# Second unit's weight splits and mixed operands queued behind the first half's normalisation, and the forget gates' chain moved to a later down product, in a hybrid decoder trunk

## The chip, the core and the metric

One NeuronCore of a Trainium2 chip runs the whole program in one launch. The metric is the device time of one execution in microseconds (us). Engines: PE (TensorE, matmul), DVE (VectorE), ACT (ScalarE), POOL (GpSimd), and SP (SyncE), which here only issues DMAs.

## What is computed

Sixteen learned meta tokens and 512 input tokens, 528 in all, of width D = 1024 pass through two layers; each has three steps, and each step ends in a LayerNorm of (scaled residual + new part). All is float32.

```
for l in range(2):
    h = layer_norm(ALPHA*h + 0.5*swiglu(h, ffn1_wg[l], ffn1_wu[l], ffn1_wd[l]), ...)
    mix = short_conv(h, ...) if l == 0 else forgetting_attention(h, w_q, w_o, k, v, c)
    h = layer_norm(ALPHA*h + mix, ...)
    h = layer_norm(ALPHA*h + 0.5*swiglu(h, ffn2_wg[l], ffn2_wu[l], ffn2_wd[l]), ...)
    if l == 0: k, v, c = shared_kv(h, kv_w, f_bias)  # c = cumsum(log_sigmoid(h @ w_f + f_bias))
```

`swiglu(x) = (silu(x @ wg) * (x @ wu)) @ wd` has 2816 inner columns. `short_conv` multiplies one projection of x by a 3-tap convolution of the product of two others. The attention has 8 heads of 128; its scores get c[query] - c[key] added before the softmax.

## The kernel before

**Layout.** The residual `y` stays in SBUF, transposed: features on the partitions (8 blocks of 128), tokens along the free axis. Tokens are worked on in two halves, h = 0 and 1, of 264 columns each (256 in layer 1, where the meta tokens are gone).

**Exact products.** A float32 product is made of three fast ones. Each operand is split in a high part (rounded, `wh`, `xh`) and the rest (`wl`, `xl`); `gemms` (L232) issues wl·xh, wh·xl and wh·xh for each block of 128 features and then calls `tick()`, which runs what `later(n, ...)` has put off by n such ticks. For weights ACT makes `wh` (a copy, L127) and DVE makes `wl` (a subtraction, L129) in `split_w`; for activations ACT and DVE do the same in `split_x` (L250). Weights are loaded by SP into three `raw` buffers of 1 MB and split into five pairs `wh`, `wl`; the first tiles of some stages have homes of their own (`xtile`) so that they can be made early.

**FFN stages.** A `Quads` holds a pair of 256-column blocks of wg and wu, cut into quarters a11 to a22. A `Unit` (L507) computes the pair for both halves at once with seven products p1 to p7 in place of eight (a Strassen form), from sums of weight quarters (`Quads.sums`, L186: s, s2, s3 on DVE; s4 at L205) and mixed operands t1 to t4 of the activations (`Mixed.sums`, L308, on DVE and ACT). These need both halves of the tokens. So the first unit after a norm can be `Direct` (L571): eight plain products, half 0 first, then half 1, with two activations each out of PSUM (`sg`, L648). `run_units` (L592) runs the Direct unit's two halves, then p1, p2, p5 and so on of the second unit. Direct first units stand at the start, in the second FFN of both layers, and in the keys and values; the first FFN of layer 1 follows the keys without a norm between. `finish` ends a unit, `down` (L477) multiplies by wd and adds to `y`.

**Norm.** `Norm.pre` takes the first feature block as a shift (`first`, a matmul, `shift` six ticks later); `add` adds each down product to `y` (L495, DVE), squares it (L400, ACT; three buffers `sq`) and accumulates sums and squares on POOL (L404, L406). `post(h)` runs for each half a few ticks after its last block: two matmuls (L414) sum over the partitions into `pd` and `pv`, then `finish`, under a priority higher than what is traced around it, runs a chain on DVE: variance (L425), an inverse root by iterations (`rsqrt`, L345 to L353), then for each pair of blocks a multiply and an add (L433, L434, DVE), gain and bias (L437, ACT) and the split (`self.to.made`, L251 and L252). The last `xl` goes into the list `newest`.

**What sets the order.** TensorE's instructions run as they are traced (`manual_schedule`). The order of DVE, ACT, POOL and SP is made at build time by the Tile scheduler: of the instructions whose inputs are there, the one traced first, with the norm's chain ahead. `behind()` (L111) holds an instruction until the newest `xl` traced so far has been issued; every `wl` and every weight sum is made under it:

```
def behind():
    return tc.issue_after(newest[-1].ins) if newest else nullcontext()
```

Within `down` of a stage with a norm, `ahead()` (at n == 2*LEAD) splits the next stage's first weights before the norm begins: a11, a21, a12, a22 of the Direct unit, blocks 0 of w_in[1] and w_in[2] for the convolution, q_w(0) and q_w(1) for the queries. In `post`, once half 1's finish is traced, `self.to.sums()` follows: for a `Mixed` the second unit's a11, a12 and s1 and all of t1 to t4; for a `Plain` (the inputs of the convolution and the queries) nothing.

**Stages in order.** Start (transposes of x, first FFN of layer 0), convolution (`conv_u`, `conv_b`, written out for the first two blocks as (u,0,0), (u,1,0), (b,0,0), (u,0,1), (b,0,1), (u,1,1), (b,1,0), (b,1,1), where a u is 48 matmuls and a b is 24), its down product, second FFN, keys and values (`kv_direct`, L833, then units), in whose second unit `gates` (L844) runs the whole chain of the forget gates (8 x 528 elements on DVE, L874 to L888, then the store of `c_dram` on POOL's queue), first FFN of layer 1, queries (`project`: heads 0 to 2 and 3, 4 for half 0, then 0 to 2 for half 1) and attention, its down product, last FFN with the output norm. `turn_c` turns c into columns for the scores, 160 ticks after the keys.

## Time and profile before

| | |
|---|---|
| median of 3 runs | 1967.3 us (1965.5 to 1967.4) |
| the profiled execution: time / span | 1965.4 / 1963.6 us |
| TensorE busy | 1886.4 us, 96%, 14467 matmuls |
| VectorE / ScalarE / GpSimd busy | 1401.3 (71%) / 876.1 (45%) / 133.6 us (7%) |
| mean granted TensorE clock | 0.985 of full speed |
| chain that ended last, by engine | PE 86%, DVE 9%, ACT 2%, issue, DMA and POOL 1% each |
| HBM traffic | 96 GB/s over the span |

The span runs from the first to the last instruction of the profiled execution; the device time has about 2 us around it. A row of an engine "in order of time" gives the start, the duration, the line, the tiles (written <- read), their shapes and, in brackets, the engine's idle time before it and what ended that. In the tables of waits an idle time is put down to the event that came last.

### The profile page before, as it was taken

The numbers are of one execution on the slowest core, as the hardware profiler recorded it, in microseconds if no ns is written. First come the engines' busy times: TensorE is split into PE (matmuls) and PEld (weight loads), VectorE is DVE, ScalarE is ACT, GpSimd is POOL, SyncE is SP. The second block draws the span as 40 slices with busy tenths as digits, with TensorE's granted clock in tenths as the row PEclk, the third lists the DMA queues.
The fourth block names the chain that finished last, engine by engine and source line by source line (L and its number), as shares of the span: only waits on it lengthen the run. The fifth ranks groups of instructions, "written<-read, shape, count | busy, mean of one in ns | idle before, by whom it ended". The sixth has DMA issues, their size and how long they took to land.

```text
span 1963.6 us, 34602 instructions
## 1 busy us (share of the span) xinstructions
PE 1886.4 (96%) x14467; PEld 1822.4 (93%) x14467; DVE 1401.3 (71%) x2077; ACT 876.1 (45%) x1459; POOL 133.6 (7%) x198
## 2 busy tenths in 40 slices
PE   8999999979998999999899999999979989999997
PEld 7999999879998999999899998989968888989897
DVE  6686767754478776767899875858658787858685
ACT  5353535433245353535454453535435544535360
POOL 0000000400031000000421000000300220000000
PEclk9999999989999999999999999999979999999999
DMA  4333323222230332323233323333413302333241
GB/s 143 119 99 96 108 87 108 65 97 84 100 97 18 123 108 87 108 87 110 85 110 131 108 89 105 98 101 109 146 54 116 102 1 97 103 109 102 96 130 44
DMA packets 180682, 190.43 MB, mean 97 GB/s; under 512 B 5834, under 2 KB 174070, under 8 KB 180526
## 3 DMA queue, kind: packets, MB, share of 16 engines
q1 hardware_dynamic: 178510, 182.74, 29.1%
q0 software_dynamic: 2016, 5.49, 0.8%
q8 instruction: 113, 1.85, 0.4%
q14 instruction: 43, 0.35, 0.1%
HBM read 181.76 MB, written 6.44 MB: 96 GB/s over the span
## 4 chain that ended last, share of the span: by engine, by line
PE 86%; DVE 9%; ACT 2%; issue 1%; DMA 1%; POOL 1%; SPq 0%; DVEq 0%; ACTq 0%; POOLq 0%
PE pb L238 26%; PE pc L238 15%; PE pa L238 6%; PE pcv L238 2%; PE pcc L238 2%; PE pcb L238 2%; PE pq L238 2%; DVE wl L129 1%; DVE xl L252 1%; DVE y L433 1%; DVE y L434 1%; PE psc L953 1%; PE po L1011 1%; ACT y L437 1%; PE pt L708 0%
## 5 line engine op out<-in xcount | busy, mean ns | idle before, releaser
L129 DVE TENSOR_TENSOR wl<-raw,wh 128x1024 fp32r<-128x1024 f32 (+1 forms) x440 | 518.8, 1185 | 201.2 <-ACT wh L127 187.1
L127 ACT CAST wh<-raw 128x1024 fp32r<-128x1024 f32 (+1 forms) x440 | 439.2, 1003 | 480.9 <-PE pc L238 74.0
L238 PE MATMUL pb<-xh,wl 128*128 128x264 f32 (+1 forms) x1408 | 400.8, 285 | 11.0 <-ACT sg L648 11.0
L238 PE MATMUL pb<-xh,wh 128*128 128x264 f32 (+1 forms) x1408 | 400.2, 284 | 0.0
L238 PE MATMUL pb<-xl,wh 128*128 128x264 f32 (+1 forms) x1408 | 400.0, 284 | 0.0
L238 PE MATMUL pc<-xh,wl 128*128 128x264 f32 (+1 forms) x960 | 273.8, 285 | 7.4 <-DVE wl L129 6.4
L238 PEld LDWEIGHTS pb<-xh,wl 128*128 128x128 f32 x1408 | 266.9, 190 | 11.8 <-ACT sg L648 11.4
L238 PE MATMUL pc<-xl,wh 128*128 128x264 f32 (+1 forms) x960 | 272.9, 284 | 3.4 <-DVE xl L252 3.4
L238 PE MATMUL pc<-xh,wh 128*128 128x264 f32 (+1 forms) x960 | 272.4, 284 | 0.0
L238 PEld LDWEIGHTS pb<-xh,wh 128*128 128x128 f32 x1408 | 267.8, 190 | 0.0
L238 PEld LDWEIGHTS pb<-xl,wh 128*128 128x128 f32 x1408 | 266.9, 190 | 0.3
L238 PEld LDWEIGHTS pc<-xh,wl 128*128 128x128 f32 x960 | 181.4, 189 | 8.4 <-DVE wl L129 3.9
L238 PEld LDWEIGHTS pc<-xl,wh 128*128 128x128 f32 x960 | 181.5, 189 | 4.5 <-DVE xl L252 4.5
L238 PEld LDWEIGHTS pc<-xh,wh 128*128 128x128 f32 x960 | 181.8, 189 | 0.0
L238 PE MATMUL pa<-xh,wl 128*128 128x264 f32 (+1 forms) x352 | 99.7, 283 | 0.0
L238 PE MATMUL pa<-xh,wh 128*128 128x264 f32 (+1 forms) x352 | 99.6, 283 | 0.0
L238 PE MATMUL pa<-xl,wh 128*128 128x264 f32 (+1 forms) x352 | 99.5, 283 | 0.0
L127 ACT CAST wh<-s 128x1024 fp32r<-128x1024 f32 x44 | 46.1, 1047 | 48.4 <-DVE s L194 7.9
L238 PEld LDWEIGHTS pa<-xh,wh 128*128 128x128 f32 x352 | 66.3, 188 | 0.0
L238 PEld LDWEIGHTS pa<-xh,wl 128*128 128x128 f32 x352 | 66.2, 188 | 0.0
L238 PEld LDWEIGHTS pa<-xl,wh 128*128 128x128 f32 x352 | 66.2, 188 | 0.0
L437 ACT ACTIVATE y<-y,vecs 128x264 f32<-128x264 f32 (+1 forms) x80 | 43.9, 597 | 45.1 <-DVE y L434 45.1
(1919 smaller groups left out, 4558.5 us busy)
## 6 DMA issues: line engine op xcount, KB each, us to landing
raw<-in_ffn_wg_dram SPq DMA_DIRECT2D x88, 512.0 KB, 3.8
raw<-in_ffn_wu_dram SPq DMA_DIRECT2D x88, 512.0 KB, 4.8
raw<-in_ffn_wd_dram SPq DMA_DIRECT2D x48, 768.0 KB, 4.5
raw<-in_conv_w_in_dram SPq DMA_DIRECT2D x12, 1024.0 KB, 4.9
raw<-in_ffn_wd_dram SPq DMA_DIRECT2D x16, 512.0 KB, 3.6
raw<-in_kv_w_dram SPq DMA_DIRECT2D x16, 512.0 KB, 4.7
raw<-in_conv_w_out_dram SPq DMA_DIRECT2D x4, 1024.0 KB, 5.4
raw<-in_attn_w_q_dram SPq DMA_DIRECT2D x4, 1024.0 KB, 6.7
```

Source lines behind the costliest of these rows:

```text
L127: nc.scalar.copy(a, src)
L129: nc.vector.tensor_tensor(b, src, a.bitcast(F32), ALU.subtract)
L238: nc.tensor.matmul(ps, lhsT=a[:, k, :], rhs=b(k), start=start and k == ks[0] and j == 0, stop=stop and k == ks[-1] and j == 2, skip_group_ ...
L252: return nc.vector.tensor_tensor(dst_l, src32, dst_h.bitcast(F32), ALU.subtract)
L433: nc.vector.tensor_tensor(ym, ym, rb, ALU.mult)
L434: nc.vector.tensor_tensor(ym, ym, bb, ALU.add)
L437: nc.scalar.activation(yv[:, j, :], yv[:, j, :], AF.Identity, scale=vecs[:, c:c + 1], bias=vecs[:, 48 + c:49 + c])
L953: nc.tensor.matmul(ps, lhsT=q[:, M + t * P:M + (t + 1) * P], rhs=kt[:, a:b], start=True, stop=True)
L1011: nc.tensor.matmul(po[:, q0:S], lhsT=vt[:, j * P:(j + 1) * P], rhs=pT[j // 2][:, j % 2, q0:S], start=j == 0, stop=False)
```

## The change

1. `behind()` takes the instructions to wait for; `split_x` returns ACT's copy and DVE's subtraction.
2. `Norm.post` calls `self.to.early()` after half 0's finish in place of `self.to.sums()` after half 1's. For a `Mixed`, `early` makes the second unit's a11, a12 and the weight sums (with a11 split before the sums overwrite it); for the convolution it splits w_in[1](1), w_in[2](1) and w_in[0](0), for the queries heads 2, 3 and 4.
3. `Mixed.sums` (t1 to t4 and the split of s1) is called by `run_units` between the Direct unit's two halves, behind the last split pair of half 0's output (in the keys behind ACT's last copy); t3 is split at once, t4 is written in t2's place. `turn_x` no longer calls it at the start. For this, `ready` becomes a list of two `Quads`.
4. `shift` comes eight ticks after `first`, not six, and `sq` has four buffers, not three.
5. The gates' chain becomes `forget()`, 232 ticks after the gates' matmuls; it works in `c_keep` and copies the result there at the end. `turn_c` comes 320 ticks after the keys, not 160.

```diff
...
@@ -108,9 +108,14 @@
     newest = []
-    def behind():
-
-        return tc.issue_after(newest[-1].ins) if newest else nullcontext()
+    @contextmanager
+    def behind(*after):
+
+
+        with ExitStack() as stack:
+            for ins in after or newest[-1:]:
+                stack.enter_context(tc.issue_after(ins.ins))
+            yield
     def split_w(src, shape, home=None):
@@ -186,6 +191,7 @@
         def sums(self):
             if "s" in self.got:
                 return
+            self("a11")
             s = wp.tile([P, KD * P], F32, tag="ws", bufs=1, name="s")
             s = s.rearrange("p (j k n) -> p j k n", j=2, k=KH)
             self.got["s"] = s
@@ -248,16 +254,17 @@
             finish()
     def split_x(dst_h, dst_l, src32):
-        nc.scalar.copy(dst_h, src32)
-        return nc.vector.tensor_tensor(dst_l, src32, dst_h.bitcast(F32), ALU.subtract)
+        a = nc.scalar.copy(dst_h, src32)
+        return a, nc.vector.tensor_tensor(dst_l, src32, dst_h.bitcast(F32), ALU.subtract)
     class Plain:
-        def __init__(self, layer):
+        def __init__(self, layer, early):
             self.layer = layer
             self.q = {}
+            self.early = early
         def made(self, h, m):
@@ -270,9 +277,6 @@
             k = m % KH
             return split_x(a[:, k:k + 2, :w], b[:, k:k + 2, :w], yv[:, m:m + 2, :])
-        def sums(self):
-            pass
-
         def operands(self, h):
             w = SPAN[self.layer][h][1]
             return tuple(
...
@@ -305,15 +309,19 @@
             i, k = m // KH, m % KH
             return split_x(*self.tiles(f"b{i + 1}{h + 1}", k), self.part(i, h, k))
+        def early(self):
+
+
+            self.left("a11")
+            self.left("a12")
+            self.left.sums()
+
         def sums(self):
-
             b = self.part
             w = self.w
             new = lambda n: gtile(n, 2 * w).rearrange("p (k c) -> p k c", k=2)
             t = {}
-            self.left("a11")
-            self.left("a12")
             for k in range(0, KH, 2):
                 t1 = new("t1")
                 nc.vector.tensor_tensor(t1, b(0, 0, k), b(0, 1, k), ALU.subtract)
@@ -324,13 +332,11 @@
                 nc.vector.tensor_tensor(t3, b(1, 1, k), b(0, 1, k), ALU.subtract)
                 nc.vector.scalar_tensor_tensor(t2, b(0, 0, k), -1.0, t3, ALU.mult, ALU.subtract)
                 split_x(*self.tiles("t2", k), t2)
-                t[k] = t2, t3
+                split_x(*self.tiles("t3", k), t3)
+                t[k] = t2
             for k in range(0, KH, 2):
-                split_x(*self.tiles("t3", k), t[k][1])
-            for k in range(0, KH, 2):
-                t4, t2 = new("t4"), t[k][0]
-                nc.vector.scalar_tensor_tensor(t4, t2, -1.0, b(1, 0, k), ALU.mult, ALU.subtract)
-                split_x(*self.tiles("t4", k), t4)
+                nc.vector.scalar_tensor_tensor(t[k], t[k], -1.0, b(1, 0, k), ALU.mult, ALU.subtract)
+                split_x(*self.tiles("t4", k), t[k])
         def __getitem__(self, name):
             if name == "b12":
@@ -385,7 +391,7 @@
                 for m, gather in self.early.pop(h, ()):
                     self.add(h, m, gather)
-            later(6, shift)
+            later(8, shift)
         def add(self, h, m, gather):
@@ -396,7 +402,7 @@
             yv = cols(y, h, self.layer)
             if m == 1:
                 self.s1[h] = self.tmp(h, "s1")
-            sq = self.tmp(h, "sq", 3)
+            sq = self.tmp(h, "sq", 4)
             nc.scalar.activation(sq, yv[:, m, :], AF.Square)
             if m == KD - 1:
                 self.sq[h] = sq
@@ -414,8 +420,8 @@
                     nc.tensor.matmul(ps, lhsT=ones_all, rhs=t, start=n == 0, stop=n == 1)
             with tc.high_priority(offset=SOON):
                 self.finish(h, pd, pv)
-            if h == 1:
-                self.to.sums()
+            if h == 0:
+                self.to.early()
         def finish(self, h, pd, pv):
             yv = cols(y, h, self.layer)
@@ -438,7 +444,7 @@
                         yv[:, j, :], yv[:, j, :], AF.Identity,
                         scale=vecs[:, c:c + 1], bias=vecs[:, 48 + c:49 + c])
                 last = self.to.made(h, m)
-            newest.append(last)
+            newest.append(last[1])
     def lagged(n, head, layer, group=1, tail=0):
@@ -584,7 +590,8 @@
                         gemms([(ps[j, m], (wh[:, j], wl[:, j]), self.xs[f"b{n + 1}{h + 1}"])],
                               range(KH), start=n == 0, stop=n == 1, chained=True)
             for m in range(2):
-                finish(m, h, ps[0, m], ps[1, m])
+                last = finish(m, h, ps[0, m], ps[1, m])
+            return last
     def first_four(quads):
         return lambda: [quads(n) for n in ("a11", "a21", "a12", "a22")]
@@ -594,9 +601,12 @@
         if direct:
-            units[0].xs.left = units[1].quads
+            xs = units[0].xs
             for h in range(2):
-                units[0].half(h, direct)
+                last = units[0].half(h, direct)
+                if h == 0:
+                    with behind(*last):
+                        xs.sums()
             if after:
                 after(0)
         i0 = int(direct is not None)
...
@@ -647,14 +660,13 @@
                 sg = gtile("sg", w)
                 nc.scalar.activation(sg, pg, AF.Silu)
                 nc.vector.tensor_tensor(sg, sg, pu, ALU.mult)
-                split_h(m, h * w, sg)
+                return split_h(m, h * w, sg)
             units = []
             for i in range(fn // 2):
                 c0 = (f0 + 2 * i) * P
-                fresh = ready and not (c or i)
-                q = ready if fresh else Quads([a[:, c0:c0 + 256] for a in (wg, wu)])
-                if not fresh:
+                q = ready[i] if ready and c == 0 else pair_quads(wg, wu, c0)
+                if not ready or c or i:
                     units.append(Unit(q, xs, [lambda m: gtile("g"), lambda m: gtile("u")]))
                 else:
                     units.append(Direct(q, xs))
...
@@ -712,9 +725,6 @@
             nc.scalar.copy(y[:, m, c0:c0 + w], ps[:, :w])
             if m % 2:
                 xs0.made(h, m - 1)
-        if h == 1:
-            xs0.sums()
-
     def turn_vecs():
         ps = psum("pvec")
         nc.tensor.transpose(out=ps[:, :120], in_=vr, identity=ident[:120, :120])
@@ -726,11 +736,11 @@
     later(8 * KD, turn_vecs)
-    xc = Plain(0)
     w_in = [Weights(conv_w_in[0], 0, KD, j * D, KD) for j in range(3)]
     for j in (1, 2):
         w_in[j].home = {0: xtile}
-    ffn(0, ffn1_wg[0], ffn1_wu[0], ffn1_wd[0], 0, xs0, xc, ready=first,
+    xc = Plain(0, lambda: (w_in[1](1), w_in[2](1), w_in[0](0)))
+    ffn(0, ffn1_wg[0], ffn1_wu[0], ffn1_wd[0], 0, xs0, xc, ready=f1,
         ahead=lambda: (w_in[1](0), w_in[2](0)))
     zh, zl = {}, {}
@@ -790,15 +800,15 @@
         o, w = SPAN[0][h]
         return (lambda k: zh[k][:, o:o + w]), (lambda k: zl[k][:, o:o + w])
-    xs1 = Mixed(0)
-    f2 = Quads([a[0][:, :256] for a in (ffn2_wg, ffn2_wu)], xtile)
+    f2 = [pair_quads(ffn2_wg[0], ffn2_wu[0], c, None if c else xtile) for c in (0, 256)]
+    xs1 = Mixed(0, f2[1])
     down(0, Weights(conv_w_out[0], 0, KD, 0, KD), KD, z_operands, True,
-         Norm(0, 1, EPS, xs1), ALPHA, ahead=first_four(f2))
-
-    xs2 = Mixed(0)
+         Norm(0, 1, EPS, xs1), ALPHA, ahead=first_four(f2[0]))
+
     kv_quads = [
         Quads([kv_w[:, j * D + i * 256:j * D + (i + 1) * 256] for j in range(2)], None if i else xtile)
         for i in range(H // 2)]
+    xs2 = Mixed(0, kv_quads[1])
     ffn(0, ffn2_wg[0], ffn2_wu[0], ffn2_wd[0], 2, xs1, xs2, ready=f2, ahead=first_four(kv_quads[0]))
@@ -835,9 +845,10 @@
         for j, ps in enumerate(pss):
             if h == 0:
                 kv0[j, m] = htile("kvT", F32)
-            nc.scalar.copy(kv0[j, m][:, o:o + w], ps)
+            last = nc.scalar.copy(kv0[j, m][:, o:o + w], ps)
         if h == 1:
             kv_store(0, m, kv0[0, m], kv0[1, m])
+        return [last]
     c_keep = nrm.tile([H, T], F32, name="c_keep")
@@ -858,7 +869,7 @@
         nc.vector.tensor_tensor(fl[:, :, 0:H], fr, fh[:, :, 0:H].bitcast(F32), ALU.subtract)
         nc.vector.tensor_scalar(fn[:, :, 0:H], fh[:, :, 0:H].bitcast(F32), -1.0, None, ALU.mult)
         nc.vector.tensor_scalar(fm[:, :, 0:H], fl[:, :, 0:H].bitcast(F32), -1.0, None, ALU.mult)
-        z, e, q, q2, acc = (gtile(n)[:H] for n in ("z", "e", "q", "q2", "acc"))
+        z = c_keep
         low = lambda a, b: (a[:, :KH], b[:, :KH])
         high = lambda a, b: (a[:, KH:], b[:, KH:])
@@ -870,6 +881,11 @@
             for n, (wt, name) in enumerate(parts):
                 gemms([(ps, wt, xs2[name])], range(KH), start=n == 0, stop=n == len(parts) - 1)
             nc.vector.tensor_scalar(z[:, o:o + w], ps[:H, :], fbias, None, ALU.add)
+        later(29 * KD, forget)
+
+    def forget():
+        z = c_keep
+        e, q, q2, acc, c = (gtile(n)[:H] for n in ("e", "q", "q2", "acc", "c"))
         nc.scalar.activation(e, z, AF.Abs)
         nc.scalar.activation(e, e, AF.Exp, scale=-1.0)
@@ -884,7 +900,8 @@
         nc.vector.tensor_scalar(z, z, 0.0, None, ALU.min)
         nc.vector.scalar_tensor_tensor(z, acc, -2.0, z, ALU.mult, ALU.add)
         nc.vector.memset(e, 1.0)
-        nc.vector.tensor_tensor_scan(c_keep, e, z, 0.0, ALU.mult, ALU.add)
+        nc.vector.tensor_tensor_scan(c, e, z, 0.0, ALU.mult, ALU.add)
+        nc.vector.tensor_copy(z, c)
         nc.gpsimd.dma_start(c_dram, c_keep)
     kv_units = []
@@ -901,12 +918,12 @@
                 out=pt[:, :H], in_=c_keep[:, M + t * P:M + (t + 1) * P], identity=ident[:H, :H])
             nc.vector.tensor_copy(cqT[:, t, :], pt[:, :H])
-    later(20 * KD, turn_c)
-
-
-    xq = Plain(1)
+    later(40 * KD, turn_c)
+
+
     q_w = Weights(attn_w_q[0], 0, KD, 0, H)
     q_w.home = {m: xtile for m in range(2)}
+    xq = Plain(1, lambda: [q_w(m) for m in range(2, 5)])
     ffn(1, ffn1_wg[1], ffn1_wu[1], ffn1_wd[1], 3, xs2, xq, ahead=lambda: (q_w(0), q_w(1)))
     opened = {}
...
```

## Rows read from the trace of the kernel before

**Rows 1.** Busy time by stretch: start:end length, PE, PEld, DVE, ACT, POOL, clock, DMA, GB/s
```profile
420.00:540.00 120.00, 120.00 (x990) 120.00 (x990) 52.76 (x90) 37.51 (x64) 0.50 (x5) 1.00 0.26 89
1120.00:1140.00 20.00, 20.00 (x120) 17.61 (x119) 11.59 (x17) 5.91 (x7) 0.00 (x0) 1.00 0.17 53
1140.00:1180.00 40.00, 40.00 (x334) 40.00 (x334) 34.47 (x45) 23.28 (x36) 0.00 (x0) 1.00 0.29 93
```

**Rows 2.** TensorE's waits over the span: us in all, how often, the longest
```profile
PE pq L238 <- DVE wl L129: 12.9, 2, 7.9
...
PE pcc L238 <- DVE wl L129: 10.8, 1, 10.8
PE pc L238 <- DVE wl L129: 6.4, 2, 3.6
...
PE pc L374 <- ACT first L370: 3.3, 4, 2.3
```

**Rows 3.** TensorE in order of time: first matmuls behind its waits
```profile
404.28 0.59 PE L238 MATMUL pcc<-xh,wl 128*128 128x264 f32 x1 [10.77 <-DVE wl L129]
404.67 0.42 PE L238 MATMUL pcc<-xl,wh 128*128 128x264 f32 x1
404.89 0.42 PE L238 MATMUL pcc<-xh,wh 128*128 128x264 f32 x1
...
623.41 0.59 PE L238 MATMUL pb<-xh,wl 128*128 128x264 f32 x1 [4.75 <-ACT sg L648]
...
1053.32 0.39 PE L238 MATMUL pc<-xh,wl 128*128 128x264 f32 x1 [3.63 <-DVE wl L129]
...
1449.50 0.58 PE L238 MATMUL pq<-xh,wl 128*128 128x256 f32 x1 [7.91 <-DVE wl L129]
...
1623.25 0.58 PE L238 MATMUL pb<-xh,wl 128*128 128x256 f32 x1 [6.25 <-ACT sg L648]
```

**Rows 4.** DVE in order of time, around the second norm of each boundary
```profile
389.60 0.43 DVE L425 SCALAR_TENSOR_TENSOR v<-pv,v 128x264 f32<-128x264 f32 x1 [1.55 <-PE pv L414]
...
398.35 0.70 DVE L252 TENSOR_TENSOR xl<-y,xh 128x528 fp32r<-128x528 f32 x1
...
403.01 4.63 DVE L129 TENSOR_TENSOR wl<-raw,wh 128x1024 fp32r<-128x1024 f32 x4
...
596.18 0.43 DVE L425 SCALAR_TENSOR_TENSOR v<-pv,v 128x264 f32<-128x264 f32 x1 [3.48 <-PE pv L414]
...
606.17 0.70 DVE L319 TENSOR_TENSOR t<-y 128x528 f32<-128x528 f32 x1
606.78 0.70 DVE L252 TENSOR_TENSOR xl<-y,xh 128x528 fp32r<-128x528 f32 x1
...
970.22 0.43 DVE L425 SCALAR_TENSOR_TENSOR v<-pv,v 128x264 f32<-128x264 f32 x1 [1.56 <-PE pv L414]
...
1434.94 0.42 DVE L425 SCALAR_TENSOR_TENSOR v<-pv,v 128x256 f32<-128x256 f32 x1 [5.09 <-PE pv L414]
...
1448.23 3.49 DVE L129 TENSOR_TENSOR wl<-raw,wh 128x1024 fp32r<-128x1024 f32 x3
...
1595.11 0.42 DVE L425 SCALAR_TENSOR_TENSOR v<-pv,v 128x256 f32<-128x256 f32 x1 [2.25 <-PE pv L414]
```

**Rows 5.** DVE in order of time, inside the forget gates' chain
```profile
1042.60 1.21 DVE L195 TENSOR_TENSOR raw<-raw 128x1024 f32<-128x1024 f32 x1
1043.74 0.69 DVE L882 SCALAR_TENSOR_TENSOR acc<-acc,q 8x528 f32<-8x528 f32 x1
```

**Rows 6.** DVE and POOL in order of time: side by side, and POOL by itself
```profile
561.37 5.04 DVE L129 TENSOR_TENSOR wl<-raw,wh 128x1024 fp32r<-128x1024 f32 x3
563.60 3.44 POOL L406 TENSOR_TENSOR s<-s,sq 128x264 f32<-128x264 f32 x2
...
592.93 2.38 POOL L406 TENSOR_TENSOR s<-s,sq 128x264 f32<-128x264 f32 x3
```

**Rows 7.** DVE by line, 1026 to 1051 us: busy us, mean ns | idle before
```profile
L877 DVE RECIPROCAL q<-q 8x528 f32<-8x528 f32 x1 | 3.4, 3441 | 0.0
```

More of the change, by code (lines that the diff above doesn't have):

```diff
@@ L1 @@
 import math
-from contextlib import ExitStack, nullcontext
+from contextlib import ExitStack, contextmanager
 import concourse.bass as bass
@@ L281, in trunk_kernel, with __init__ @@
     class Mixed:
-        def __init__(self, layer):
-            self.layer = layer
+        def __init__(self, layer, left=None):
+            self.layer, self.left = layer, left
             self.w = SPAN[layer][0][1]
@@ L618, in run_units, with pair_quads @@
                 nxt.p2()
+    def pair_quads(wg, wu, c0, home=None):
+        return Quads([a[:, c0:c0 + 256] for a in (wg, wu)], home)
     def ffn(layer, wg, wu, wd, ln, xs, to, last=None, ready=None, ahead=None):
@@ L630, in split_h @@
                 n = src.shape[1]
-                split_x(hh[j][:, o0 + a:o0 + a + n], hl[j][:, o0 + a:o0 + a + n], src)
+                return split_x(hh[j][:, o0 + a:o0 + a + n], hl[j][:, o0 + a:o0 + a + n], src)
             def finish(i, u, split_h=split_h):
@@ L676, in trunk_kernel @@
     ctx.enter_context(tc.manual_schedule(engines={mybir.EngineType.PE}))
-    xs0 = Mixed(0)
-    first = Quads([a[0][:, :256] for a in (ffn1_wg, ffn1_wu)], xtile)
+    f1 = [pair_quads(ffn1_wg[0], ffn1_wu[0], c, None if c else xtile) for c in (0, 256)]
+    xs0 = Mixed(0, f1[1])
+    first = f1[0]
     half = D // 2
@@ L1063, in trunk_kernel @@
     mix(7)
-    xs3 = Mixed(1)
-    f4 = Quads([a[1][:, :256] for a in (ffn2_wg, ffn2_wu)], xtile)
-    down(1, o_w, KD, o_operands, True, Norm(1, 4, EPS, xs3), ALPHA, opened, first_four(f4))
+    f4 = [pair_quads(ffn2_wg[1], ffn2_wu[1], c, None if c else xtile) for c in (0, 256)]
+    xs3 = Mixed(1, f4[1])
+    down(1, o_w, KD, o_operands, True, Norm(1, 4, EPS, xs3), ALPHA, opened, first_four(f4[0]))
     def last(w, kn, operands):
```

## The prediction, made before the changed kernel was run

> **What bounds the kernel.** I read stretches of the span first, then the waits of TensorE, then each boundary in order of time. Through the long middles of the stages TensorE never stops: 990 matmuls in 120 us of the conv stage, 0.12 us each [rows 1]. So only the waits are for sale [rows 2], and they sit where one stage's normalisation feeds the next: conv after the first FFN (near 400 us), second FFN (600), keys and values (980), queries (1440), last FFN (1600). There the residual is normalised in two halves of columns; the first half feeds TensorE while VectorE (DVE) works on the second.
>
> Three patterns matter. **Split weights come late**: at conv TensorE idles 10.77 us until `wl` exists [rows 3]; DVE makes four `wl` at 403.01, straight after the second norm that began at 389.60 [rows 4], although they need nothing of it: `behind()` ties each to the newest norm traced. At the queries it is 7.91 us, ended by the `wl` at 1448.23 [rows 3, 4]. **A bank is not released**: 4.75 and 6.25 us in the second and last FFN until `sg` is read out of PSUM [rows 3]; the mixed sums, traced before both direct halves, keep ACT and DVE from it. **DVE is full of the forget gates**: 3.63 us at 1053 [rows 3].
>
> After such a wait the clock matters too. Behind 10.77 us a matmul takes 0.42 us and starts every 0.22 [rows 3], half rate (1.2 GHz), for some 25 matmuls; 25 x 0.10 = 2.5 us more. The first matmul after 4.75, 6.25 and 7.91 us also shows the longer 0.58 or 0.59; after 3.63 us it shows 0.39, full rate (2.4 GHz) [rows 3].
>
> **The change, part by part.** All sums are against the profiled execution: span 1963.6 us, 1965.4 with what lies around it, 0.1% under the median of 1967.3.
>
> (a) *Conv.* Three splits, w_in[1](1), w_in[2](1), w_in[0](0), now hang on half 0's last `xl`. The row of four gives 1.15 us each [rows 4]: 3.5 us. Their ACT copies and loads stay as they were. DVE had 1.55 us free before the second norm; the rest enters its chain, so that half 1 is about 2 us later. That costs nothing: from 393.5, where TensorE stopped, conv_u(1,0) and conv_b(0,0) are 72 matmuls, 8.7 us, to 402.2; half 1's first `xl`, at 398.35 before, is there by 401.2 even so. Gain 10.8 + 2.5 = 13.3. The cover is those 72 matmuls; without it the 2 us would show.
>
> (b) *Queries.* q_w(2) was already behind half 0 and stays; heads 3 and 4 move before the second norm. DVE idles 5.09 us there [rows 4]; two splits are 2.3. Nothing is delayed, and heads 3 and 4 (48 matmuls, 5.8 us) carry TensorE from 1441.6 to 1447.4, about when half 1 is complete. Gain 7.9 + 2.3 = 10.2.
>
> (c) *Sums behind half 0* (second FFN, keys and values, last FFN, and the start). Both halves' `sg` now precede or mix with the t operands, so the banks are free by the end of the direct halves. Gain 4.75 + 2.5 and 6.25 + 2.4, together 15.9. At the start and at the keys no such wait exists: 0, covered by the 5.8 us (48 matmuls) of p1 and p2 before p5 needs t1.
>
> (d) *Splits and sums of the second unit before the second norm.* This is the price. Five wide DVE operations, 5 x 1.15 = 5.7 us, become ready at half 0's last `xl`. The second norm has precedence but is a chain, and a chain link lets in one waiting operation: between two links of the forget gates stands a 1.21 us add of lower standing [rows 5]. So I take all five as running before or inside the chain. Their loads are traced one norm earlier, on SP behind the same down weights as before. Gaps absorb 3.48, 1.56 and 2.25 us [rows 4]. POOL's last statistics run beside them: three `wl` beside POOL took 5.04 us and two POOL adds 3.44, against 1.15 and 0.8 each alone [rows 4, 6]; each add still to come at DVE's last `xl` (three, under one, two in POOL's order of time) costs DVE 0.5. Filled links save about 0.5 (an unrelated operation overlaps the one before by 0.1: 606.17 lasts 0.70, the next starts 0.61 later), and the t1 subtraction that stood before the second `xl` (606.17, 606.78) is gone: another 0.5. Second FFN: 5.7 + 1.5 - 1.0 - 3.5 = 2.7; keys: 5.7 + 0.3 - 1.0 - 1.6 = 3.4; last FFN: 5.7 + 1.0 - 1.0 - 2.3 = 3.4. TensorE already waits for that norm at these places, so all 9.5 are lost. Bounds: 0 (all fits the gaps) and 17 (nothing absorbed); I take the sum of rows. The wait at the keys becomes over 4 us, nearer 4.75 than 3.63, so I charge one fall of the clock, 2.5; the other two stay nearer 3.63.
>
> The page "SBUF — State Buffer" of the Trainium skill (section "SBUF: two separate sides") speaks against this part: the port pair of DVE and POOL is an exclusive lock, the loser blocked for a whole instruction. By it each add would cost DVE its full 0.8, and the loss would be 1.7 us larger; 5.04 us for three `wl` [rows 6] is most of that, not all, and I keep the row.
>
> (e) *Forget gates.* Some 14 us of DVE (one 3.44 us reciprocal, seven links of 0.69, others [rows 5, 7]) leave 1026 to 1051, and the 3.63 us wait goes with them. They return 232 ticks later, which counting ticks puts near 1120, in the first down product of layer 1, with a copy of 0.4. DVE is busy 11.6 of the 20 us to 1140 and 34.5 of the 40 after [rows 1], leaving 13.9 for 14.4: it fits, barely. TensorE never stops there now, and a late weight shows only once its lead is used up, so I take 0; at worst the 6 us that do not fit before 1140; below 0 nothing, since there is no wait to remove. The store of c moves with them on POOL's queue, behind the last key and value stores, and its readers are issued by the attention, a stage later. Gain 3.6.
>
> (f) *shift two ticks later, a fourth sq buffer.* TensorE waits 3.3 us in four places for `first`, 2.3 in one [rows 2]; two ticks are six matmuls, 0.7 us: 0.7 there and the other 1.0, 1.7 at most. Later statistics may give 0.5 back (bounds -1 and +1.7): 1.2.
>
> Sum: 13.3 + 10.2 + 15.9 + 3.6 + 1.2 = 44.2, less 9.5 and 2.5: 32.2. 1965.4 - 32.2 = 1933.
>
> **The rivals.** *No delay of the second norm* (the five fit the gaps): the 12 of (d) come back, 1921. For it: 3.48 us idle at one place; against: 1.56 at another. Chance 0.12.
>
> *DVE becomes the bound at p5.* In the second FFN, from the second norm's start at 596.18 to p5 at 618.7 + 2.7 + 5.8 = 627.2, DVE has 31.0 us for the norm (13.4, as 389.60 to 403.01), what is left of the five (2.2), eight `sg` operations (0.43 as L425, 3.4), 16 t operations (0.61 apart, 9.8) and s1's split (1.2): 30.0 [rows 4]. With 1.0 to spare, fillers make p5 wait: 3 us in each of three places with a fall of the clock, 3 x 5.5, gives 1950. Against it: work that is ready is chosen in the order it was traced, and t1 comes early in it. Chance 0.14.
>
> *The clock falls after every new wait*, as it did after 4.75 us: two falls more than mine, 5 us, 1938. Against it: full rate after 3.63 [rows 3]. Chance 0.12. The page "TensorE: Matmul & The Clock Gate" of the Trainium skill (section "Part 1: The HAM clock gate") has the clock fall to half when the engine has been idle; the 4.75 us row agrees, the 3.63 us row does not.
>
> *Slower: the second norm keeps precedence whole.* Then DVE runs the five only behind it. Conv and queries gain nothing, since their splits stand where they stood; at p5 the five (5.7) and the gated t operations come one after the other: 30.0 + 3.5 = 33.5 us for the 28.3 to p5 at 624.5, and with wide fillers between them up to 5 x 1.15 more: 5 to 11 us late plus 2.5, in three places, 23 to 40 lost against 20.7 from (c), (e) and (f). It decides from p5 being 6 us late on; middle value 1976. Against it: the add between two links [rows 5]. Chance 0.06.
>
> *It does only part of what it says* (one of conv and queries still waits, or the gates' backlog reaches TensorE): 1943 to 1964, chance 0.06, over half of it near no gain.
>
> **The numbers.** The forecast, 1933, has 0.50; its own range is 1926 to 1941. To hold eight in ten I reach to both neighbours: 1920 to 1951. A measurement of this kernel can tell 0.2%, 3.9 us, from no change. Faster 0.90, same 0.04, slower 0.06.
>
> **What would show it.** Right: no `wl` wait above 1 us at conv and one of 5 us, not two, at the queries; no wait for `sg`; the `xl` waits before the second direct half grown from 0.8 to between 2 and 4.5 us, with wide operations between links L345 to L353; no wait at the gates; `acc` rows after 1110. Wrong: p5 (`pc`) waiting for `xl` or `wl`; wide operations only behind the second norm; matmul durations of 0.42 after each `xl` wait; ACT or TensorE waits beside the gates' new place.

## The result, and the profile after

The changed kernel takes 1947.0 us (median of 4 runs, 1943.8 to 1948.6) against 1966.4 (4 runs, 1964.9 to 1967.4): ratio 0.990, interval 0.9883 to 0.9917, 19.4 us faster. The forecast was 1933, 32.2 us less, with the range 1920 to 1951. Single executions of one kernel lie up to 7 us apart below, so a difference of some 2 us between two medians proves nothing by itself. The profiled execution took 1946.8 us, span 1945.0: 18.6 less than before.

TensorE's waits over the span of the changed kernel (waited for: us, times, longest; answers to [rows 2]):

```profile
PE pq L244 <- DVE wl L134: 5.5, 1, 5.5
PE pd L420 <- DVE y L501: 5.5, 2, 5.3
PE pc L244 <- ACT xh L257: 5.4, 3, 2.3
...
PE pd__783 L244 <- ACT hh L257: 2.8, 1, 2.8
PE pc L244 <- DVE wl L134: 2.8, 1, 2.8
PE pc L380 <- ACT first L376: 2.4, 1, 2.4
PE pv L420 <- POOL s L412: 2.3, 1, 2.3
```

The 10.8 at the convolution, the 11.0 for `sg`, the second wait of the queries and the 3.6 at the gates are gone. New or longer are y in the second FFN (5.3 us for 0.3), xh in front of the second direct half (2.0 and 2.3), hh at the start (2.8), `first` at the convolution's down product (2.4) and POOL's s in the last FFN (2.3 for 0.8). Their places, from TensorE in order of time (answers to [rows 3]):

```profile
74.53 0.39 PE L244 MATMUL pd__783<-hh,wl 128*128 128x264 f32 x1 [2.82 <-ACT hh L257]
...
552.43 0.39 PE L380 MATMUL pc<-first,ones_pre 128*128 128x264 f32 x1 [2.40 <-ACT first L376]
...
593.89 1.25 PE L420 MATMUL pd<-y,ones_all 128*128 128x264 f32 x2 [5.32 <-DVE y L501]
...
978.44 0.39 PE L244 MATMUL pc<-xh,wl 128*128 128x264 f32 x1 [2.02 <-ACT xh L257]
...
1591.94 0.43 PE L244 MATMUL pc<-xh,wl 128*128 128x256 f32 x1 [2.30 <-ACT xh L257]
1592.83 0.58 PE L244 MATMUL pc<-xl,wh 128*128 128x256 f32 x1 [0.45 <-DVE xl L258]
```

TensorE's order is the same in both kernels but for a few single matmuls, so the start of the same matmul in both says where time was won:

| matmul | before | after | won (+) or lost since the line above |
|---|---|---|---|
| convolution's first (pcc) | 382.42 | 390.11 | -7.7 |
| its first conv_b (pcb) | 413.00 | 406.87 | +13.8 |
| down product behind half 0's statistics, second FFN (A) | 578.79 | 574.88 | -2.2 |
| second FFN's first down product behind hh (B) | 650.71 | 645.91 | +0.9 |
| as A, before the keys (C) | 953.08 | 948.48 | -0.2 |
| gates' first (pf) (D) | 1016.94 | 1017.92 | -5.6 |
| keys' p5 that waited for wl (pc) | 1053.32 | 1050.43 | +3.9 |
| queries' first (pq) | 1422.69 | 1416.43 | +3.4 |
| first scores (psc) | 1466.27 | 1449.71 | +10.3 |
| as A, last FFN (E) | 1578.27 | 1562.44 | -0.7 |
| as B, last FFN (F) | 1653.86 | 1635.20 | +2.8 |

They add up to 18.7. Convolution, queries and gates came as forecast, and so did the loss at the keys (5.6 for 3.4 + 2.5). The start lost 7.7 where nothing was forecast, and the second and the last FFN won 0.9 and 2.8 where some 4.6 and 5.2 were forecast. The -2.2 in front of A is the wait of 2.40 at 552.43.

### The profile page after: what moved, and what is told of

It reads as the page before. It is cut to its first block, busy times and chain, and to the rows that moved or that the text cites. A ratio compares the mean times of both kernels' runs of the same rounds, so it can differ in the third digit from the quotient of the medians.

```text
span 1945.0 us, 34609 instructions
## 1 busy us (share of the span) xinstructions
PE 1884.8 (97%) x14467; PEld 1820.9 (94%) x14467; DVE 1404.0 (72%) x2078; ACT 873.9 (45%) x1459; POOL 136.7 (7%) x198
## 4 chain that ended last, share of the span: by engine, by line
PE 84%; DVE 9%; DMA 2%; ACT 2%; POOL 1%; issue 1%; SPq 0%; DVEq 0%; ACTq 0%; POOLq 0%
PE pb L244 25%; PE pc L244 16%; PE pa L244 6%; PE pq L244 2%; PE pcc L244 2%; PE pcv L244 2%; PE pcb L244 2%; DVE wl L134 2%; DMA raw<-in_ffn_wu_dram 2%; PE psc L970 1%; PE po L1028 1%; DVE y L439 1%; POOL s L410 1%; ACT y L443 1%; POOL s L412 1%
## 5 line engine op out<-in xcount | busy, mean ns | idle before, releaser
L132 ACT CAST wh<-s 128x1024 fp32r<-128x1024 f32 x44 | 46.0, 1046 | 49.0 <-DVE s L200 10.8
L200 DVE TENSOR_TENSOR s<-raw 128x1024 f32<-128x1024 f32 x44 | 54.2, 1232 | 15.5 <-DMA raw<-in_ffn_wu_dram 13.8
(1920 smaller groups left out, 4539.8 us busy)
```

What stands on the lines that cost most here:

```text
L132: nc.scalar.copy(a, src)
L200: nc.vector.tensor_tensor(s, a21, a22, ALU.add)
```

## The experiments

Edits are shown against the changed kernel, in part. "Start as before" is part of all runs named so, of those with the add first and of those by place. A trace is of one execution, a median of four or more.

**The start.** Where did 7.7 us go? The edit:

```diff
+        if h == 1:            # turn_x
+            xs0.early()
+            xs0.sums()
...
-                if h == 0:    # run_units
+                if h == 0 and "t1" not in xs.q:
```

> Only the start goes back: the first stage's splits of a11 and a12, its weight sums and t1 to t4 are traced with the second half's transposes and wait for nothing of half 0's output; everything else is the changed kernel (1947.0 us, profiled span 1945.0). Theory A (the gate on half 0's output leaves DVE idle for some 10 us at the start, and the backlog reaches the first down product): all 7.7 us by which the first norm's matmuls come later than before return, so about 1939.3 us, and the 2.8 us wait for hh and the 1.2 us wait at s2 are gone. Rival B (the 7.7 us come from the later shift and the order of the weight loads in the first FFN, not from the gate): the waits stay, 1945 to 1948 us.

Measured: 1940.3 us (1939.2 to 1944.0), 6.7 less; the convolution's first matmul at 382.91 and no wait for hh or at s2. Theory A holds. DVE of the changed kernel in order of time, and below ACT:

```profile
27.38 0.71 DVE L258 TENSOR_TENSOR xl<-y,xh 128x528 fp32r<-128x528 f32 x1 [0.24 <-ACT xh L257]
32.03 0.43 DVE L662 TENSOR_TENSOR sg<-sg,pc 128x264 f32<-128x264 f32 x1 [3.94 <-PE pc L244]
...
34.95 0.43 DVE L662 TENSOR_TENSOR sg<-sg,pc 128x264 f32<-128x264 f32 x1 [1.58 <-PE pc L244]
...
36.21 1.32 DVE L327 TENSOR_TENSOR t<-y 128x528 f32<-128x528 f32 x2
```
```profile
72.90 1.04 ACT L132 CAST wh<-raw 128x1024 fp32r<-128x1024 f32 x1 [3.23 <-DMA raw<-in_ffn_wu_dram]
73.85 0.63 ACT L257 CAST hh<-g 128x528 fp32r<-128x528 f32 x1
```

The first t1 comes at 36.21; before the change it came at 22.88. From 28.1 to 36.2 DVE works 1.6 us. The work left over holds the `raw` tiles longer: the load of the next weights is issued at 65.6 in place of 60.6 (60.8 in the run with the old start), ACT's copy of them waits 3.23 us, and behind it in ACT's queue stands the copy hh, for which TensorE waits 2.82 us. Behind that wait the granted clock is 0.50 from 76.7 to 80.0.

**The second norms.** Two runs leave fewer wide operations ahead of them. First (only the splits a11, a12), then (none; `late` is called in half 1's `post`):

```diff
             self.left("a12")
-            self.left.sums()
```


> Of the five wide DVE operations ahead of the second norm (second FFN, keys, last FFN) only the splits of a11 and a12 stay there; the three weight sums go behind half 0's output, with the mixed operands. Theory A (the wide operations stand in DVE's queue ahead of half 1's last add and between the links of the chain, and are lost there one by one): the changed kernel loses 5.3, 5.7 and 5.9 us at the three second norms, 16.9 in all; three of five removed give back 3 x 1.15 a place or more, 10 to 14 us in all, 1933 to 1937 us. Rival B (the loss is contention of DVE and POOL, which the two splits already cause): 1 to 3 us come back, 1944 to 1946 us. Rival C (DVE is the bound at p5: the sums are only lost there instead): new waits at p5 for wl or xl, 1943 to 1950 us.


```diff
         def early(self):
+            self.left.load(0)
+            self.left.load(1)
+        def late(self):
             self.left("a11")
             self.left("a12")
-            self.left.sums()
```


> None of the five wide operations stays ahead of the second norm: the second unit's weights are loaded as early as in the changed kernel, but a11 and a12 are split behind half 1's last xl, as before the change, and the sums stand behind half 0's output. Theory A (order in DVE's queue): the second norms are as early as before the change, all 16.9 us come back, 1930 us, unless p1 waits for a11; then 3 us less. Rival B (contention): the same 1930 us, since nothing runs beside POOL any more; it differs from A in the run with two operations early. Rival C (DVE is the bound at p5): the five operations of 1.15 us, 5.7 us a place, come back as waits at p1 or p5 with a fall of the clock each: 1945 to 1955 us.

Measured: 1945.6 (1945.0 to 1947.5) and 1940.9 us (1939.3 to 1946.0; the profiled execution is the slowest). Neither gave what A forecast; the first lies in the ranges of B and C, the second in none. The stretches of the table above, in us, of one profiled execution each:

| kernel | second FFN, A to B | keys, C to D | last FFN, E to F |
|---|---|---|---|
| before | 71.9 | 63.9 | 75.6 |
| changed | 71.0 | 69.4 | 72.8 |
| two early | 73.7 | 64.9 | 70.8 |
| none early | 71.8 | 65.0 | 72.6 |
| start as before, add first | 71.4 | 69.0 | 71.9 |
| the same, two early | 71.5 | 65.7 | 69.1 |

The same traces say when the second norm ran. "Start" is the time from the stretch's first matmul to the first DVE operation of the norm's chain (v, L431 in the changed kernel), "chain" the time from there to b (L435), in us:

| kernel | second FFN: start, chain | keys: start, chain | last FFN: start, chain |
|---|---|---|---|
| before | 17.4, 4.1 | 17.1, 4.1 | 16.8, 4.0 |
| changed | 23.0, 4.1 | 18.4, 7.1 | 17.9, 7.2 |
| two early | 21.1, 4.1 | 18.3, 4.1 | 17.8, 4.0 |
| none early | 17.4, 4.1 | 18.3, 4.1 | 16.8, 4.0 |
| start as before, add first | 20.1, 6.1 | 19.4, 7.1 | 18.2, 8.1 |
| the same, two early | 19.2, 4.1 | 19.1, 4.1 | 17.8, 4.0 |

Where the chain is longer, wide operations stand between its links (DVE of the changed kernel at the keys):

```profile
966.85 0.42 DVE L431 SCALAR_TENSOR_TENSOR v<-pv,v 128x264 f32<-128x264 f32 x1
967.19 1.21 DVE L200 TENSOR_TENSOR s<-raw 128x1024 f32<-128x1024 f32 x1
968.32 0.28 DVE L351 TENSOR_SCALAR r<-v 128x264 int32<-128x264 int32 x1
968.53 1.21 DVE L201 TENSOR_TENSOR raw<-raw 128x1024 f32<-128x1024 f32 x1
969.66 0.42 DVE L353 TENSOR_TENSOR a<-r 128x264 f32<-128x264 f32 x1
970.00 1.21 DVE L202 TENSOR_TENSOR raw<-raw,s 128x1024 f32<-128x1024 f32 x1
971.14 0.42 DVE L354 SCALAR_TENSOR_TENSOR a<-a,v 128x264 f32<-128x264 f32 x1
...
973.94 0.43 DVE L435 SCALAR_TENSOR_TENSOR b<-pd,r 128x264 f32<-128x264 f32 x1
```

With none early the second norm is back where it was, as A says (at the keys but for a fall of the granted clock at 964.2). With two early it is back but for what those two cost the start, 3.7 us in the second FFN. At the keys that gives back 4.5 us of the stretch. In the two FFNs the sums behind half 0 come back as waits: with two early the last FFN keeps 2.0 us of the 3.2 that its chain gives back, and the second FFN is 2.7 longer; with none early TensorE waits for `sg` again, now at p5 (TensorE, none early; then two early):

```profile
626.53 0.59 PE L244 MATMUL pc<-xh,wl 128*128 128x264 f32 x1 [3.56 <-ACT sg L664]
```
```profile
632.42 0.36 PE L244 MATMUL pb<-xh,wl 128*128 128x264 f32 x1 [1.23 <-DVE wl L134]
...
646.81 0.39 PE L244 MATMUL pd__7127<-hh,wl 128*128 128x264 f32 x1 [2.10 <-ACT hh L257]
```

So A is right on the norm, and C (the sums are lost behind it instead) on what follows it in the FFNs; at the keys, where no `sg` and no hh are wanted, A stands alone. In the second FFN of the changed kernel something else is seen (DVE, then POOL; answers to [rows 6]):

```profile
588.37 3.44 DVE L134 TENSOR_TENSOR wl<-raw,wh 128x1024 fp32r<-128x1024 f32 x2
591.74 1.76 DVE L200 TENSOR_TENSOR s<-raw 128x1024 f32<-128x1024 f32 x1
593.42 0.41 DVE L501 TENSOR_TENSOR y<-y,pd__6553 128x264 f32<-128x264 f32 x1
...
597.89 0.43 DVE L431 SCALAR_TENSOR_TENSOR v<-pv,v 128x264 f32<-128x264 f32 x1 [1.45 <-PE pv L420]
```
```profile
589.02 5.07 POOL L412 TENSOR_TENSOR s<-s,sq 128x264 f32<-128x264 f32 x3
```

Half 1's last add (593.42) stands behind three wide operations, though its product was done at 586.7; and beside them POOL's three adds take 5.07 us, not 2.38 [rows 6]. Which of the two makes the norm late? The next run puts the add first:

```diff
-            gather()
+            if h == 1 and m == KD - 1:
+                with tc.high_priority(offset=SOON):
+                    gather()
+            else:
+                gather()
```


> The start as before the change (that run alone: 1940.3 us), and in each norm the last residual add of half 1 (the write of y by line L501, block 7) gets precedence on DVE, so that the splits and weight sums of the second unit can't stand ahead of it. Theory A (in the second FFN the second norm is late because this add of 0.4 us stands behind three wide operations): TensorE's 5.3 us wait for y at the second FFN is gone, the chain starts when POOL's sums are there, and what is left of the five operations goes between the links, as at the keys: 2 to 4 us gained, 1936 to 1938 us; keys and last FFN as they were, since their adds already ran first. Rival B (DVE and POOL slow each other, and POOL's sums set the norm's start wherever the add is): the wait moves from y to POOL's s with the same length, 1939 to 1941 us.

Measured: 1944.9 us (1940.6 to 1946.5; the profiled execution is the fastest), above both ranges and 4.6 more than the start as before alone. The add runs at 584.26, and the wait passes on to POOL, as in B, but not at the same length (TensorE, then POOL):

```profile
590.04 0.71 PE L424 MATMUL pv<-s,ones_all 128*128 128x264 f32 x2 [3.70 <-POOL s L416]
```
```profile
584.91 5.08 POOL L416 TENSOR_TENSOR s<-s,sq 128x264 f32<-128x264 f32 x3
```

So both made the norm late. Of the 5.6 us by which its start had moved, 2.9 were the late add (23.0 to 20.1) and the 2.7 left are what POOL's adds take longer (5.08 for 2.38). The gain is lost again: two wide operations now go between the links (chain 6.1), as A had it, and in the convolution, where the edit applies too, TensorE waits 1.43 us for POOL's sums in place of 0.51 and the way from its first matmul to its first conv_b is 19.3 us, not 16.8.

Both edits together (add first, two early):

> As the run with the add first, and only the splits of a11 and a12 ahead of the second norm (the weight sums behind half 0's output). Theory A: the keys give back 4.5 us and the last FFN 2.0 as in the run with two operations early, and the second FFN, which lost 2.7 there to a late add and the backlog behind it, is no worse than in the run with the add first: 1930 to 1933 us. Rival C (the sums behind half 0's output keep DVE busy until p7 and the down product, whatever the norm does): waits for wl at s3 and for hh come back in the second FFN with a fall of the clock, 1934 to 1939 us.

Measured: 1937.1 us (1934.3 to 1940.0), C's range: the waits at s3 (1.20) and for hh (1.76) are back in the second FFN; keys and last FFN are short.

**Parts taken out alone.** Convolution and queries (`xc`, `xq` with an empty `early`), then the gates' chain at its old place:

```diff
-    xc = Plain(0, lambda: (w_in[1](1), w_in[2](1), w_in[0](0)))
+    xc = Plain(0, lambda: None)
-    xq = Plain(1, lambda: [q_w(m) for m in range(2, 5)])
+    xq = Plain(1, lambda: None)
```


> The three weight splits of the convolution and heads 2 to 4 of the queries are no longer made ahead of the second norm; all else is the changed kernel. Theory A (this part alone gave 13.8 us at the convolution and 10.3 at the queries): the waits of about 10.8 and 7.9 us return, 1947.0 + 24.1 = 1971 us, slower than the kernel before. Rival B (the later shift or the fourth sq buffer gave part of it): the waits return smaller, 1960 to 1966 us.


```diff
-        later(29 * KD, forget)
+        forget()
-    later(40 * KD, turn_c)
+    later(20 * KD, turn_c)
```


> The forget gates' chain runs directly behind its matmuls again, turn_c 160 ticks behind the keys; all else is the changed kernel (1947.0 us). Theory A (the chain's 14 us of DVE cost TensorE 3.6 us at the second to third unit of the keys, and nothing at the new place): the wait for wl near 1050 returns, 1950.6 us. Rival B (at the new place the chain costs as much, hidden in small waits of the down product): no difference, 1946 to 1948 us. Rival D (the changed kernel's DVE is later here, so the chain costs more than before): 1952 us or more.

Without the early splits: 1969.9 us (1968.5 to 1974.7), slower than before (ratio 1.0019, 1.0009 to 1.0029); the waits are 10.78 and 7.90 us again. A holds. With the gates at the old place: 1953.6 us (1952.6 to 1955.0), 6.6 more, so D: the wait is little longer than before, but TensorE now restarts at half rate (0.59, not 0.39 as in [rows 3]):

```profile
1054.70 0.59 PE L244 MATMUL pc<-xh,wl 128*128 128x264 f32 x1 [3.98 <-DVE wl L134]
```

**Shift and buffers.** Alone, then with the start as before:

```diff
-            later(8, shift)
+            later(6, shift)
-            sq = self.tmp(h, "sq", 4)
+            sq = self.tmp(h, "sq", 3)
```


> The shift comes six ticks behind first again, and sq has three buffers; all else is the changed kernel (1947.0 us). Theory A (both only move waits for first about: a new one of 2.4 us at the convolution's down product, one of 2.3 us with a fall of the clock gone at the first FFN of layer 1): the first goes, the second returns, 1948 to 1949 us. Rival B (the two ticks are worth 0.7 us in each of six norms): 1950 to 1951 us. Rival E (the wait at the convolution is the whole of it): 1944.6 us.

> The start as before the change (that run alone: 1940.3 us), and shift after six ticks with three sq buffers. The run with shift and buffers alone gained 5.0 us on the changed kernel; its trace puts 3.7 of them in the first FFN, where nothing of shift or sq had run yet: there ACT waited 1.65 us for a weight load in place of 3.23. Theory A (those 3.7 us are the loads of the hurried start, not the shift): with the start unhurried only 0 to 2 us are left, 1938 to 1940 us. Rival B (shift and buffers are worth the 5 us): 1935 us.

Measured: 1942.0 us (1941.7 to 1944.9), 5.0 less, below all three forecasts; and 1939.5 (1937.0 to 1941.9), 0.8 less than the start alone, as A had it. ACT and TensorE of the first run, in order of time:

```profile
71.00 1.04 ACT L132 CAST wh<-raw 128x1024 fp32r<-128x1024 f32 x1 [1.65 <-DMA raw<-in_ffn_wu_dram]
```
```profile
542.52 0.39 PE L380 MATMUL pc<-first,ones_pre 128*128 128x264 f32 x1 [0.75 <-ACT first L376]
```

One part is firm: with eight ticks every kernel waits 2.1 to 2.6 us for `first` at the convolution's down product (552.43 above) and some 0.7 for POOL at the first FFN's norm; with six, 0.8 to 1.0 and nothing (the kernel before: at most 0.2 and nothing). With eight, `first` at the convolution stands in ACT's queue behind a weight copy that waits for its load (ACT of the changed kernel):

```profile
550.39 1.04 ACT L132 CAST wh<-raw 128x1024 fp32r<-128x1024 f32 x1 [2.15 <-DMA raw<-in_ffn_wu_dram]
551.34 0.73 ACT L406 ACTIVATE sq<-y 128x264 f32<-128x264 f32 x2
551.98 0.40 ACT L376 CAST first<-y 128x264 fp32r<-128x264 f32 x1
```

The other part depends on when loads land. In the first run the wait for the load in the first FFN is 1.6 us shorter, though SP's order is the same; in the second TensorE waited 2.0 us for `first` at the queries' down product, as it had before the change, since ACT stood 4.70 us in front of the queries' weights:

```profile
1376.69 1.99 ACT L132 CAST wh<-raw 128x1024 fp32r<-128x1024 f32 x2 [4.70 <-DMA raw<-in_attn_w_q_dram]
1379.36 0.41 ACT L376 CAST first<-y 128x256 fp32r<-128x256 f32 x1 [0.68 <-DVE y L505]
```

**Put together.** By place (start as before; weight sums early only in the second FFN); with it the queries' head 2 split ahead of the first norm; with both, six ticks and three buffers:

```diff
-            self.left.sums()
+            if self.sums_early:       # true for xs0 and xs1
+                self.left.sums()
```


> The start as before, all five early operations in the second FFN, and only the splits of a11 and a12 early at the keys and in the last FFN. Theory A (each place keeps what its own stretch showed: the keys shorter by 3.7 us and the last FFN by 1.5 than in the run with the start alone): 1935 us. Rival C (DVE's backlog moves on to the next stage and is paid there): 1938 to 1941 us.


```diff
-    q_w.home = {m: xtile for m in range(2)}
+    q_w.home = {m: xtile for m in range(3)}
...
-    ahead=lambda: (q_w(0), q_w(1)))
+    ahead=lambda: (q_w(0), q_w(1), q_w(2)))
```


> As the run by place, and the queries' head 2 is split with heads 0 and 1 ahead of the first norm, with tiles of its own. Theory A (the 5.5 us wait for wl at head 2, which the change left, and the fall of the clock behind it, 1.2 us, are the gate on half 0's last xl alone): both gone, 6.5 us under the run by place, 1928 to 1929 us. Rival B (the split only moves in front of the first norm's chain, and delays it by as much as a split takes): 1930 us. Rival C (TensorE then waits at the heads of half 0 for something else, as long): no gain.

> As the run before, with shift after six ticks and three sq buffers. Theory A (the two are worth 0 to 2 us): 1926 to 1929 us. Rival B (5 us): 1923 to 1924 us.

Measured: 1934.4 (1929.5 to 1935.9), A; 1932.0 (1931.7 to 1935.8), 2.4 less in place of 6.5, between the forecasts of B and C; and 1927.2 us (1926.1 to 1930.6), 4.8 less still: in A's range, but by a step of B's size, since the run before it had come out above its forecast. In the second the wait of 5.5 us is gone and the stretch from the queries' first matmul to the block behind the norm's is 7.6 us, not 12.3, but TensorE waits 1.74 us for POOL's sums just before. The last one is faster than the kernel before and than the changed one: ratio 0.980 to the kernel before, interval 0.9784 to 0.9813.

## Why the prediction was right and wrong

The measured time lies in the range of 1920 to 1951, but outside the forecast's own narrower one (1926 to 1941): the profiled execution won 18.6 us of 32.2, 58%. Of the 13.6 us that are missing 7.7 stand at the start, which the sum had at 0, and some 3.7 and 2.4 in the second and the last FFN; the rest cancels.

(a) **Convolution**: 13.8 for 13.3; the 72 matmuls did cover the later second half. (b) **Queries**: 10.3 for 10.2. Taking both out cost 22.8.

(c) **Banks**: the waits for `sg` went, as forecast. The step that failed is "At the start and at the keys no such wait exists: 0, covered by the 5.8 us (48 matmuls) of p1 and p2 before p5 needs t1". p5 was covered. What was left out is that the gate itself stops DVE at the start, where it had been working ahead, and that the backlog is paid later, at s2 (1.2 us), in the loads and at hh (2.8 and 1.0, then half the clock): 7.7 us in all, of which the run with the old start gave back 6.7.

(d) **Second norms**: the links did let in wide operations one by one, as read from [rows 5]. At the keys and in the last FFN the chain started 1.2 and 1.0 us later and grew by 3.0 and 3.2: 4.2 each for the 3.4 forecast. In the second FFN the start alone came 5.6 us later, for 2.7. There the step that failed is "Gaps absorb 3.48, 1.56 and 2.25 us": DVE's own time was not what set the start. DVE still idled 1.45 us in front of the chain (597.89), while the norm waited for TensorE's sums, and those for the late add (2.9 us) and for POOL (2.7). That each add of POOL costs DVE 0.5 held: a wide operation takes 1.76 us beside POOL (591.74) and 1.21 without it (967.19). What had no term is what DVE costs POOL, whose three adds took 5.07 us for 2.38.

The Trainium skill ("SBUF — State Buffer", section "SBUF: two separate sides") has one of the two engines blocked for a whole instruction. In the sum the trace is near it: the three wide operations and the three adds took from 588.4 to 594.1, 5.7 us, and alone they take 3.5 [rows 4] and 2.4 [rows 6]. For DVE it is not: 0.55 us an add, not the whole 0.8 that the prediction worked out by that rule.

The fall of the clock charged at the keys came, though behind waits of 2.02, 0.55 and 0.85 us, not behind the one of over 4 that it was charged for. Four more came that were not charged: at the start (76.7), at the keys before the second norm (960.97), in the second FFN (granted clock 0.50 from 592.0 to 598.9) and in the last FFN (0.58 at 1592.83).

(e) **Gates**: 3.9 in the table for 3.6; at the new place nothing waits longer than 0.3 us. The store of c leaves at 1133. Taken out of the changed kernel the move is worth 6.6.

(f) **Shift**: forecast 1.2 gained. That two ticks are worth some 0.7 held where a wait stood before: at the queries' down product, with loads equally late (ACT waits 4.5 to 4.7 us for them), TensorE waits 1.13 us for `first` in the run by place and 2.01 in the one with the start as before and six ticks. The step that failed is that only these waits were counted: eight ticks brought a new one of 2.1 to 2.6 us at the convolution's down product, where `first` now stands behind a weight copy that waits for its load, and one of 0.7 for POOL's sums at the first FFN's norm. Of the 3.4 us won before the queries the kernel with six ticks alone keeps 2.1; so the larger part goes with the earlier landing of their weights (ACT waits 2.83 us for them, 5.04 before).

Of the rivals, "DVE becomes the bound at p5" forecast 1950, nearest to the result, but not by its mechanism: p5 waits for nothing in the changed kernel. It is nearest to what the kernels with the sums behind half 0 show, at p5 or behind it. "The clock falls after every new wait" came in both FFNs, beside larger losses that it did not name. "Slower" did not come, nor did what "only part" describes, though 1947 lies in its range.

## What to carry to other kernels

A gate that keeps low work out of the way of urgent work also stops an engine that was running ahead: count what it had done by then, and follow the backlog to the loads. Where two engines slow each other, charge both, and ask first which of the two the path waits for; an idle stretch of an engine is no room to fill when work placed in it slows what ends that stretch. One order rarely suits all places: the three weight sums ahead of the second norm cost the keys 4.5 us and saved the second FFN 2.7 (0.1 with the add first), in one execution each.

## What the hardware showed that was not expected

The same loads, issued in the same order, landed 1.5 us apart. DMA issues from 55 to 80 us (KB each, median us to landing) of the changed kernel and of the run with six ticks alone:

```profile
raw<-in_ffn_wu_dram SPq DMA_DIRECT2D x3, 512.0 KB, 6.9
```
```profile
raw<-in_ffn_wu_dram SPq DMA_DIRECT2D x3, 512.0 KB, 5.4
```

Between a wait of 3.63 us (restart at 0.39 us a matmul) and one of 3.98 (0.59) the clock's behaviour changes at the same matmul; yet after 2.30 and 0.45 us close together it fell as well. Behind the keys' first norm it fell after waits of 1.04, 0.54 and 0.58 us, where the kernel before had 1.02, 0.55 and 0.58 and kept its full rate (changed, then before):

```profile
960.97 0.59 PE L244 MATMUL pc<-xl,wh 128*128 128x264 f32 x1 [0.58 <-DVE xl L258]
```
```profile
965.55 0.39 PE L238 MATMUL pc<-xl,wh 128*128 128x264 f32 x1 [0.58 <-DVE xl L252]
```

The length of the waits alone doesn't tell it. Only one run with six ticks has the late start, so whether the six ticks had a part in its earlier loads stays open.
